# A hybrid decoder layer: four slices of feed-forward operand sums, one PSUM ring order and one set of output rows in other places

## The chip, the cores and the metric

The kernel is one program on one core of one Trainium2 chip. The metric is device time in microseconds (us) of that core, from the start of the program to its end. Lower is better. The kernel before took 2840.08, 2844.31 and 2846.90 us in three runs, with a median of 2844.31 us.

## The reference, cut to what matters

One step of one layer, for 2048 new prompt tokens and 32 sample tokens (8 sequences of 4). The model width is 1024, in fp32 throughout.

```python
def _layer(x, pos, ck, cv, s0, w_in, lb, hg_norm_w, sinks, w_up_a, w_up_b, w_o, n1, n2, w_ff1, w_ff2):
    h = _rmsnorm(x, n1)
    z = h @ w_in
    hq, hf, hi, hg, sq, sk, sv, ga, gb = jnp.split(z, ...)
    f = lb + (1.0 - lb) * jax.nn.sigmoid(hf)
    o_hg, s_new = _hgrn_recurrence(heads(hq), heads(jnp.log(f)), heads(1.0 - f), heads(hi), s0, 64)
    o_hg = _rmsnorm(o_hg, hg_norm_w)
    y_a = (o_hg * jax.nn.silu(hg)) @ w_up_a
    q, k, v = _rotary(sq, pos), _rotary(sk, pos), sv
    o_b, nk, nv = _swa_prompt(q, k, v, sinks)      # or _swa_sample with the cached keys ck and values cv
    y_b = o_b @ w_up_b
    m = jax.nn.sigmoid(ga) * y_a + jax.nn.sigmoid(gb) * y_b
    x = x + m @ w_o
    h2 = _rmsnorm(x, n2)
    x = x + jnp.square(jax.nn.relu(h2 @ w_ff1)) @ w_ff2
    return x, nk, nv, s_new
# y = _rmsnorm(x, normf_w) of both token groups; also returned: the new key and value windows and states
```

`hq`, `hf`, `hi` and `hg` have 512 columns each (4 heads of 128), `sq` 512 (8 heads of 64), `sk` and `sv` 128 each, `ga` and `gb` 1024 each; `w_ff1` is 1024 x 4096 and `w_ff2` 4096 x 1024. Attention goes over a window of 128 positions, with a sink in the softmax.

## The kernel before, in words

**Numbers.** Every fp32 product is made of three fp32r products: each operand is split into a high part (a copy on ScalarE, ACT; L257 in `split_out`, L151 in `split_in`) and a low part (a subtraction on VectorE, DVE; L258 and L152), and TensorE (PE) adds high x high, high x low and low x high in PSUM.

**Blocks and pairs.** The prompt is worked off in 4 blocks of 512 tokens; block 3 also carries the 32 sample tokens (T = 544). Blocks 0 and 1 are the first pair (`sb` = 0, half width `Ths` 512), blocks 2 and 3 the second (`sb` = 1, half width 528). The tokens lie along the free axis, the model's 1024 rows in 8 groups of 128 (`k` or `j`).

**A block.** Blocks 0 and 1 project their columns of `w_in` one after the other (`hi`, `hq`, `sq`, `skv`, and so on); the weight comes in units of two groups of 128 rows (`gemm_NK`: one unit is loaded, split and multiplied, then a hook is called). Block 2 first does `skv` and `sq` for its own tokens, whose result goes over the tiles `stg` to a DRAM buffer `zqk`, and then the **z stage**: all other projections but `hi` for blocks 2 and 3 together, by Strassen's method with seven products (below). After that blocks 2 and 3 load their part of `z` back, and do only `hi` (and block 3 its `sq` and `skv`) by themselves. Then come the window attention, interleaved by hand with the levels of the HGRN2 recurrence (`T_` rotates and transposes a tile, `S_` makes its scores, `P_` turns the probabilities, `V_` multiplies the values; `fill` issues so many matmuls of the recurrence between them), the gate loops (one over `j` for `gb` and `y_b`, "b" below, and one for `ga` and `y_a`, "a"), and `wo`, the product with `w_o`, with a list `todo` of small jobs that are called between its matmuls. In block 2, `wo`'s list holds `reload` and `recast`, which bring block 3's input back and split it. The last pieces of a block, its second norm (`n2.stat`: transposes and row sums of the squares; `n2.spread`: the factor put back on all partitions; `h2_out`: the scaled rows stored), are put into the list `late` and called by hooks (`late_at`) inside the next block's first products.

**The sample tokens** in block 3 are attended to inside its `hi`: `smp_scores`, `smp_turn` and `smp_values` hang on the hooks of units 0, 1 and 2. Their cached keys are loaded into the tile `kc` (L966), behind sixteen small stores of the new sample keys and values (L964).

**Strassen stages.** `strassen_T` runs the z stage and each pair's FF1. A `Wpair` loads a pair of weight columns (`early` the first two operands B11 and B21, `rest` the others) and splits them (`done`). A `Unit` multiplies: `a` does `fB` (into the ring `mm` or `tp`) and `fC` (into `hg`), `b` and `c` the other five, with `fD` in `sw`. The first six units run their `a` ahead of everything else. FF2 goes through seven `steps`; in each, the partial results of four groups of output rows go into PSUM banks that the table `rings` names, and `evac` (L1591) adds them to `y`.

**FF operand sums.** FF1 of the first pair needs S1 to S4, sums of the four quarters of the normed rows. For group `k`, a **slice** is: four loads of 128x512 (`ff_rows`, L583, on SP's queue) into three tiles of the tag `t4`, four sums on DVE (L602 to L608 in `ff_sums`) and four stores (L610, issued from GpSimd, POOL). Four slices make the whole. Before, slices 0 and 1 hang on the hooks of block 2's `hi` (`fr_hook`), slices 2 and 3 on those of block 3's `sq` and `skv` (`sq_fr`).

**What is shared.** PSUM has four rings of two banks, `mm`, `tp`, `hg` and `sw`. Weights go through twelve tiles of tag `w`, three for a unit (raw, high, low). The tag `t4` has three tiles, used by the slices and by the sample's `kc`, `kcT`, `vc` and `pc`. SP's queue issues the weight loads (L138), the slices' loads, `kc` and the small stores; POOL's queue issues the slices' stores and POOL also does the rotary products and the adds of the gates (L1305); ACT's queue issues the stores of `zqk` and of the z stage.

**What sets the order.** The program text is traced in order, and a list scheduler then orders the instructions of each engine by its own estimates. Two things bind it: in the attention part the order on PE is written out by hand, and `pin` (`keep_in_program_order`) keeps an instruction behind everything that was traced before it on its engine. The loads of the slices (L583) and their sums in blocks 2 and 3 are pinned.

**The end.** The second pair's FF2 ends with two pieces of 264 columns, `f1s[0]` and `f1s[1]` (class `Fin`). Each takes squares (`sq`), a statistic over PE (`stat`), the factor spread back over PE (`spread`), and eight output rows (`out`, L1445), each scaled on DVE and stored.

The functions that the diff touches, as they were:

## Time and profile before

| | before |
|---|---|
| median of three runs | 2844.31 us |
| profiled execution | 2856.07 us |
| its span in the trace | 2854.1 us |
| mean granted TensorE clock | 0.987 |
| TensorE (PE) busy | 2743.9 us, 96% |
| TensorE weight loads (PEld) busy | 2414.4 us, 85% |
| VectorE (DVE) busy | 1788.6 us, 63% |
| ScalarE (ACT) busy | 1110.6 us, 39% |
| GpSimd (POOL) busy | 489.8 us, 17% |
| moved by DMA | 487.60 MB, mean 171 GB/s |
| instructions | 50092 |

All of these but the first row are of one execution, taken by the hardware profiler. PE is TensorE's matrix products, and PEld its weight loads, which lie beside them. A wait of an engine is its idle time in front of an instruction, and the profile puts it down to the work that ended last before the instruction could start: "PE x <- ACT y" says that a matmul into tile x stood until ACT was done with y. SPq is the queue of SP, which issues DMAs. The granted clock is the share of TensorE's full clock that it got in a stretch of time. Where a row begins with two numbers, these are the start in us from the beginning of the span and the time in us of one instruction (or of the whole group, where the row ends in a count); a row of the list of waits ends in the sum of us, the number of waits and the longest.

### The profile page before, as it was taken

How to read it: one execution, taken by the hardware profiler on the slowest of the kernel's cores; microseconds unless marked ns; L12 is line 12 of the kernel's file. 1: busy time of each engine (PE TensorE's matmuls, PEld its weight loads, DVE VectorE, ACT ScalarE, POOL GpSimd, SP SyncE). 2: the span in 40 equal slices, each digit the busy share in tenths (PEclk: the TensorE clock that was granted, in tenths of full speed). 3: DMA queues.
4: the chain of work that ended last, by engine and by line, in shares of the span. 5: the costliest groups of instructions: out<-in, count | busy, mean ns of one | idle time of the engine just before them, and what ended most of it. 6: DMA issues, size and time to landing. Idle time of an engine off the chain costs nothing.

```text
span 2854.1 us, 50092 instructions
## 1 busy us (share of the span) xinstructions
PE 2743.9 (96%) x20053; PEld 2414.4 (85%) x20053; DVE 1788.6 (63%) x2905; ACT 1110.6 (39%) x2070; POOL 489.8 (17%) x782
## 2 busy tenths in 40 slices
PE   8999999999899989989899999999998999999998
PEld 7778877788799967767898888887888999999997
DVE  5675646646764375535667777765567777664556
ACT  4542445323344353324325333434443233343332
...
GB/s 187 76 107 236 206 190 67 105 235 264 231 122 113 158 91 106 211 169 51 87 196 208 161 162 159 228 320 230 195 195 205 157 144 152 146 288 187 188 187 114
DMA packets 344481, 487.60 MB, mean 171 GB/s; under 512 B 23432, under 2 KB 220824, under 8 KB 344248
## 3 DMA queue, kind: packets, MB, share of 16 engines
...
## 4 chain that ended last, share of the span: by engine, by line
PE 76%; DMA 8%; DVE 5%; issue 5%; ACT 3%; POOL 2%; SPq 0%; POOLq 0%; ACTq 0%; DVEq 0%
PE f L1585 6%; PE f L1584 6%; PE f L1586 6%; PE fB_f L264 4%; PE fB_f L266 4%; PE fB_f L265 4%; PE fD_f L264 2%; PE fD_f L266 2%; PE fD_f L265 2%; PE wob L1394 1%; PE wob L1392 1%; PE wob L1393 1%; PE fB_z L264 1%; PE fB_z L266 1%; PE fB_z L265 1%
## 5 line engine op out<-in xcount | busy, mean ns | idle before, releaser
L1584 PE MATMUL f<-f2S,hw2T 128*128 128x264 f32 (+1 forms) x576 | 184.5, 320 | 2.5 <-ACT hw2T L151 2.5
L1586 PE MATMUL f<-f2S,lw2T 128*128 128x264 f32 (+1 forms) x576 | 184.2, 320 | 1.0 <-DVE lw2T L152 1.0
L1585 PE MATMUL f<-f2S,hw2T 128*128 128x264 f32 (+1 forms) x576 | 184.1, 320 | 0.0
L264 PE MATMUL fB_f<-S,w1T_f 128*128 128x264 f32 (+1 forms) x384 | 123.0, 321 | 3.1 <-ACT c_f L327 2.5
L1584 PE MATMUL f<-f2A,h_w2B 128*128 128x264 f32 (+1 forms) x384 | 122.4, 319 | 0.0
L1585 PE MATMUL f<-f2A,h_w2B 128*128 128x264 f32 (+1 forms) x384 | 122.3, 319 | 0.0
L1586 PE MATMUL f<-f2A,l_w2B 128*128 128x264 f32 (+1 forms) x384 | 122.3, 318 | 0.0
L265 PE MATMUL fB_f<-S,w1T_f 128*128 128x264 f32 (+1 forms) x384 | 122.2, 319 | 0.0
L266 PE MATMUL fB_f<-S,w1T_f 128*128 128x264 f32 (+1 forms) x384 | 121.9, 319 | 0.0
L152 DVE TENSOR_TENSOR lw2T<-lw2T,hw2T 128x1024 fp32r<-128x1024 f32 x64 | 78.2, 1224 | 65.9 <-ACT hw2T L151 65.0
L1584 PEld LDWEIGHTS f<-f2S,hw2T 128*128 128x128 f32 x576 | 108.7, 189 | 10.5 <-ACT hw2T L151 3.0
L151 ACT CAST hw2T<-lw2T 128x1024 fp32r<-128x1024 f32 x64 | 67.2, 1051 | 128.8 <-DMA lw2T<-w_T 128.8
L1586 PEld LDWEIGHTS f<-f2S,lw2T 128*128 128x128 f32 x576 | 108.4, 188 | 9.5 <-DVE lw2T L152 1.8
L1585 PEld LDWEIGHTS f<-f2S,hw2T 128*128 128x128 f32 x576 | 108.8, 189 | 7.5
L1394 PE MATMUL wob<-m_b,l_wob 128*128 128x512 f32 (+2 forms) x320 | 112.1, 350 | 2.8 <-DVE l_wob L258 2.8
L1392 PE MATMUL wob<-m_b,h_wob 128*128 128x512 f32 (+2 forms) x320 | 112.1, 350 | 0.0
L1393 PE MATMUL wob<-m_b,h_wob 128*128 128x512 f32 (+2 forms) x320 | 111.8, 349 | 0.0
L152 DVE TENSOR_TENSOR f2S<-f2S 128x1024 fp32r<-128x1024 f32 (+1 forms) x64 | 79.0, 1240 | 43.8 <-ACT f2S L151 43.2
L258 DVE TENSOR_TENSOR w1T_f<-w1r_f,w1T_f 128x512 fp32r<-128x512 f32 x128 | 87.4, 688 | 26.2 <-ACT w1T_f L257 25.9
L257 ACT CAST w1T_f<-w1r_f 128x512 fp32r<-128x512 f32 x128 | 77.1, 619 | 65.2 <-PE fB_f L266 27.9
...
L258 DVE TENSOR_TENSOR l_w2B<-rw2B,h_w2B 128x1024 fp32r<-128x1024 f32 x48 | 58.8, 1224 | 62.6 <-ACT h_w2B L257 52.7
...
## 6 DMA issues: line engine op xcount, KB each, us to landing
...
```

What stands on the lines that cost most here:

```text
L152: pin(nc.vector.tensor_tensor(lo, F(lo), F(hi), ALU.subtract), on)
L257: pin(nc.scalar.copy(dh, src), on)
L258: pin(nc.vector.tensor_tensor(dl, src, F(dh), ALU.subtract), on)
L264: nc.tensor.matmul(ps, wh, ah, start=(first and k == 0), stop=False, skip_group_check=not first)
L265: nc.tensor.matmul(ps, wh, al, start=False, stop=False, skip_group_check=not first)
L266: nc.tensor.matmul(ps, wl, ah, start=False, stop=(last and k == 3), skip_group_check=not first)
L1392: nc.tensor.matmul(p, wh, ah, start=(k == 0), stop=False)
L1393: nc.tensor.matmul(p, wh, al, start=False, stop=False)
L1394: nc.tensor.matmul(p, wl, ah, start=False, stop=(k == KD - 1))
L1584: nc.tensor.matmul(ps, wh, ah, start=first, stop=False, skip_group_check=cont)
L1585: nc.tensor.matmul(ps, wh, al, start=False, stop=False, skip_group_check=cont)
L1586: nc.tensor.matmul(ps, wl, ah, start=False, stop=lastk, skip_group_check=cont)
```

## The change

Eleven things are edited together:

1. Slices 0 and 1 leave the hooks of block 2's `hi`. Their loads and sums are called from its gate loops, by a small table: load 0 after `j` = 0 of loop "b", its sums after `j` = 5, load 1 after `j` = 6, its sums after `j` = 3 of loop "a".
2. Slices 2 and 3 leave block 3's `sq` and `skv`. They go into the list `todo` of block 2's `wo`, between `reload` and `recast`.
3. In block 3's `hi`, `smp_turn` moves from unit 1's hook to unit 2's and `smp_values` from unit 2's to unit 3's.
4. In the attention's order by hand, the two `fill`s around the first `P_` change from 30 and 10 to 24 and 16.
5. In block 2, `sq` comes ahead of `skv`. The store of each `stg` is issued with `skv`'s part, and the hooks of `late` change with the order (`late_at(0, 2)` in `sq`, `late_at(1)` in `skv`; before, `late_at(1)` in `skv` and `late_at(0, 1)` in `sq`).
6. The first pair's FF2 uses for the four groups of its last step the rings mm, mm, hg, hg in place of hg, hg, mm, mm.
7. The last block's `n2` uses the ring `sw` in place of `hg`.
8. At the end, the output rows of the first piece `f1s[0]` leave the list `end0`. They are called behind the second piece's statistic, and are pinned there.
9. Follows from 1 and 2: each slice's loads, sums and stores now run in block 2's gate loops and `wo`.
10. In `strassen_T`, the first pair's `early` splits are pinned (`early(i == 0)`).
11. Follows from all: the order on each engine is planned anew for the new text.

`ff_sums` and `fr_sums` also get an argument for the queue of the stores, whose default is the queue used before; no call sets another.

```diff
--- before.py
+++ after.py
@@ -273,16 +273,16 @@
         def __init__(u, N, n, src, wt):
             u.N, u.n, u.src, u.wt, u.ops = f"{N}_{n}", n, src, wt, {}
 
-        def done(u, name, raw):
+        def done(u, name, raw, on=False):
             v = (u.wt if name in ("T3", "T4") else wtile)(F32R, f"w1{name}_{u.N}").rearrange("p (s k c) -> p s k c", s=2, k=4)
-            split_out(v[:, 0], v[:, 1], raw)
+            split_out(v[:, 0], v[:, 1], raw, on)
             u.ops[name] = v
 
-        def early(u):
+        def early(u, on=False):
             v = wtile(F32, f"w1r0_{u.N}").rearrange("p (s k c) -> p s k c", s=2, k=4)
             for kh in range(2):
                 nc.sync.dma_start(v[:, kh], u.src(u.n, kh)[:, 0:P].rearrange("(k p) c -> p k c", p=P))
-                u.done(f"B{kh + 1}1", v[:, kh])
+                u.done(f"B{kh + 1}1", v[:, kh], on)
 
         def rest(u):
             b = []
@@ -380,7 +380,7 @@
             units[-1].free, units[-1].ring = True, mm_ps
         for i in range(ahead):
             if i % nch == 0:
-                units[i].pair.early()
+                units[i].pair.early(i == 0)
             units[i].a(i < 4)
             early(i, units[i])
         for i, u in enumerate(units):
@@ -582,7 +582,7 @@
         for x, (r0, c0) in zip(r, ((0, 0), (4, 0), (0, Th), (4, Th))):
             pin(nc.sync.dma_start(x, h2d[b][(r0 + k) * P:(r0 + k + 1) * P, c0:c0 + Th]))
 
-    def ff_sums(b, v, r, k, loaded=False):
+    def ff_sums(b, v, r, k, loaded=False, q=nc.gpsimd):
 
 
         Th = Ths[b]
@@ -607,7 +607,7 @@
         pin(tt(a21, a11, a21, ALU.subtract), loaded)
         pin(tt(a12, a12, s2, ALU.subtract), loaded)
         for n, x in (("S2", s2), ("S1", s1), ("S3", a21), ("S4", a12)):
-            nc.gpsimd.dma_start(sd[b][n][k * P:(k + 1) * P, :], x)
+            q.dma_start(sd[b][n][k * P:(k + 1) * P, :], x)
 
     def op_load(b, v, x, r0, c0, now=True):
         out = []
@@ -828,13 +828,13 @@
 
             def st_skv(ps, kind, c, nr):
                 nc.scalar.copy(stage[c][:, 512:768], ps)
+                nc.scalar.dma_start(zqk[sb][c * P:(c + 1) * P, :], stage[c])
 
             def st_sq(ps, kind, c, nr):
                 nc.scalar.activation(qk_out(stage[c][:, 0:512]), qk_in(ps), AF.Copy, scale=HD ** -0.5)
-                nc.scalar.dma_start(zqk[sb][c * P:(c + 1) * P, :], stage[c])
-
+
+            colN512(C_SQ, f"sq{B}", st_sq, late_at(0, 2))
             colN(C_SQ + 512, f"skv{B}", st_skv, late_at(1))
-            colN512(C_SQ, f"sq{B}", st_sq, late_at(0, 1))
             Th = Ths[sb]
             r0, r1 = z_half
             A = {"A11": hT_cur[0], "A12": hT_cur[1], "S1": opT(sb, 2, "zS1"), "S2": opT(sb, 3, "zS2"), "S3": opT(sb, 6, "zS3")}
@@ -902,9 +902,11 @@
             fr.append((k, [x[:, c:c + 512] for x in r for c in (0, 512)]))
             ff_rows(0, fr[-1][1], k)
 
-        def fr_sums():
+        def fr_sums(q=nc.gpsimd):
             k, r = fr.pop()
-            ff_sums(0, None, r, k, True)
+            ff_sums(0, None, r, k, True, q)
+
+        fr_at = {("b", 0): lambda: fr_load(0), ("b", 5): fr_sums, ("b", 6): lambda: fr_load(1), ("a", 3): fr_sums} if zs and not odd else {}
 
         if not zs:
             colN512(C_HI, f"hi{B}", ev_v, *((late_at(0, 2, 3), None) if bi else (first_stat, first_split)))
@@ -912,24 +914,13 @@
                 first = bi == 0 and h < 2
                 colT(C_HQ, h, f"hq{B}{h}", ev_q, sw_ps if first else mm_ps, (lambda: spread(rb0, rs0[:, 0], bt, "first")) if first and h == 0 else None)
         if odd or not zs:
-            sq_late = late_at(0, 2, 3)
-            sq_fr = iter([lambda: fr_load(2), none, none, lambda: [fr_sums(), fr_load(3)], none, none, none, fr_sums, none] if zs else [none] * 9)
-            colN512(C_SQ, f"sq{B}", ev_sq, lambda i, ul: [sq_late(), next(sq_fr)()])
-            colN(C_SQ + 512, f"skv{B}", ev_skv, lambda: next(sq_fr)())
+            colN512(C_SQ, f"sq{B}", ev_sq, late_at(0, 2, 3))
+            colN(C_SQ + 512, f"skv{B}", ev_skv)
         else:
             for c in range(ncb):
                 nc.gpsimd.dma_start(qkv[:, c, :], zqk[sb][c * P:(c + 1) * P, :])
             nc.gpsimd.dma_start(qW, kmaj(zd[sb], 0, HH, z0 + ns, bt))
-            def fr_hook(i, ul):
-                if i == 0:
-                    fr_load(0)
-                elif i == 2:
-                    fr_sums()
-                    fr_load(1)
-                elif i == 3:
-                    fr_sums()
-
-            colN512(C_HI, f"hi{B}", ev_v, fr_hook)
+            colN512(C_HI, f"hi{B}", ev_v)
         ob = op(6, F32R, "ob_" + B)[:, 0:8 * T].rearrange("p (s k t) -> p s k t", s=2, k=4)
 
         def rotary_T(ti, nr, rr, r0, name):
@@ -1037,7 +1028,7 @@
 
         if zs and odd:
             nc.gpsimd.dma_start(qW, kmaj(zd[sb], 0, HH, z0 + ns, bt))
-            smp_at = {0: lambda: [smp_scores(kv) for kv in range(NKV)], 1: lambda: [smp_turn(kv) for kv in range(NKV)], 2: smp_values} if smp else {}
+            smp_at = {0: lambda: [smp_scores(kv) for kv in range(NKV)], 2: lambda: [smp_turn(kv) for kv in range(NKV)], 3: smp_values} if smp else {}
             colN512(C_HI, f"hi{B}", ev_v, lambda i, ul: smp_at[i]() if i in smp_at else None)
 
         kts = {-1: k_last}
@@ -1128,7 +1119,7 @@
                     n -= 1
 
         T_, S_, P_, V_ = swa_turn, swa_scores, swa_probs, swa_values
-        for f, c in ((T_, 0), (fill, 6), (S_, 0), (T_, 1), (fill, 12), (S_, 1), (T_, 2), (fill, 30), (P_, 0), (fill, 10), (V_, 0), (S_, 2), (T_, 3), (fill, 10), (P_, 1),
+        for f, c in ((T_, 0), (fill, 6), (S_, 0), (T_, 1), (fill, 12), (S_, 1), (T_, 2), (fill, 24), (P_, 0), (fill, 16), (V_, 0), (S_, 2), (T_, 3), (fill, 10), (P_, 1),
                      (fill, 10), (V_, 1), (S_, 3), (fill, 10), (P_, 2), (fill, 8), (V_, 2), (fill, 16), (P_, 3), (fill, 8), (V_, 3)):
             f(c * len(segs) if f is fill else c)
         fill(1000)
@@ -1277,6 +1268,8 @@
             if zs and j < 4:
                 nc.vector.tensor_copy(ga[:, 2 * j, 0:1], pb[:, j, 0:1])
                 nc.gpsimd.dma_start(ga[:, 2 * j:2 * j + 2, :], kmaj(zd[sb], HH + KD + 2 * j, 2, z0, T))
+            if ("b", j) in fr_at:
+                fr_at["b", j]()
             if sb == 0 and j % 2 == 1:
                 sum_next()
             elif sb == 0:
@@ -1304,6 +1297,8 @@
             for t0, n, o in gate(C_GA, j, ua, a_acts, lambda j, t0, n: ga[:, j, t0:t0 + n] if zs else t2(f"ta_{B}{j}_{t0}")[:, 0:n], "a"):
                 (nc.vector if j >= KD - 2 else nc.gpsimd).tensor_tensor(o, o, pb[:, j, t0:t0 + n], ALU.add)
                 split_out(mT[j // 4][:, 0, j % 4, t0:t0 + n], mT[j // 4][:, 1, j % 4, t0:t0 + n], o)
+            if ("a", j) in fr_at:
+                fr_at["a", j]()
 
         while side.get(bi):
             side_next(bi)
@@ -1354,7 +1349,8 @@
             def recast(g, k):
                 split_in(hT_next[g][:, 0, k:k + 2], hT_next[g][:, 1, k:k + 2], True)
 
-            todo += [lambda: [reload(0, 0), reload(0, 2)], none, lambda: recast(0, 0), lambda: [recast(0, 2), reload(1, 0)], lambda: reload(1, 2), lambda: recast(1, 0), lambda: recast(1, 2)]
+            todo += [lambda: [fr_load(2), reload(0, 0)], lambda: reload(0, 2), fr_sums, lambda: [fr_load(3), recast(0, 0)],
+                     lambda: [recast(0, 2), reload(1, 0)], lambda: [fr_sums(), reload(1, 2)], lambda: recast(1, 0), lambda: recast(1, 2)]
         else:
             Tn = Ths[sb + 1]
             hT_next = [opT(sb + 1, g, "hT") for g in range(2)]
@@ -1409,7 +1405,7 @@
                 nc.gpsimd.dma_start(h2d[sb][k * P:(k + 1) * P, z0:z0 + T], x1[:, k])
 
         if last_b:
-            n2.ring = hg_ps
+            n2.ring = sw_ps
         late += [n2.stat, n2.spread] + ([] if last_b else [h2_out])
     wk_ctx.close()
     cm_ctx.close()
@@ -1438,11 +1434,11 @@
             f.rb = f.x("rb")
             spread(f.rb, f.rs, f.ln, f.N, f.ring)
 
-        def out(f, *js):
+        def out(f, *js, on=False):
             for j in js:
                 y = f.y(j)
                 o = y if f.o is None else f.o()
-                nc.vector.scalar_tensor_tensor(o, y, nfc[:, j:j + 1], f.rb, ALU.mult, ALU.mult)
+                pin(nc.vector.scalar_tensor_tensor(o, y, nfc[:, j:j + 1], f.rb, ALU.mult, ALU.mult), on)
                 f.q.dma_start(yT[j * P:(j + 1) * P, f.c0:f.c0 + f.ln], o)
 
     f1 = None
@@ -1521,7 +1517,7 @@
         if len(chunks) == 1:
             late_ops = []
             ra, rb = (tp_ps, tp_ps, hg_ps, hg_ps), (mm_ps, mm_ps, sw_ps, sw_ps)
-            rings = (ra, rb, rb, ra, rb, rb, (hg_ps, hg_ps, mm_ps, mm_ps))
+            rings = (ra, rb, rb, ra, rb, rb, (mm_ps, mm_ps, hg_ps, hg_ps))
         else:
             rings = ((tp_ps, hg_ps, mm_ps, sw_ps),) * 6 + ((hg_ps, mm_ps, sw_ps, hg_ps),)
         last = sb == nsb - 1
@@ -1644,7 +1640,7 @@
             avs = [u_load(ao, g) for g in range(KG)]
             todo = [lambda: f0.sq(4), lambda: f0.sq(5), lambda: f0.sq(6), lambda: f0.sq(7), none, none, f0.stat, none, none, none, f0.spread]
             todo += [lambda j=j: f0.out(j) for j in range(KD)] + [lambda j=j: [f.sq(j) for f in f1s] for j in range(4, KD)]
-            end0 = [none, none, none, f1s[0].stat, none, f1s[0].spread, lambda: f1s[0].out(0, 1, 2, 3), lambda: f1s[0].out(4, 5, 6, 7)]
+            end0 = [none, none, none, f1s[0].stat, none, f1s[0].spread]
             for jp in range(2):
                 wts = []
                 for g in range(KG):
@@ -1666,6 +1662,7 @@
             while todo:
                 todo.pop(0)()
             f1s[1].stat()
+            f1s[0].out(*range(KD), on=True)
             f1s[1].spread()
             f1s[1].out(*range(KD))
 
```

## The prediction

> **What bounds the kernel now.** The page comes first: TensorE (PE) is busy for almost the whole span, so what another engine does shows in the time only where PE waits for it.
>
> ```profile
> span 2854.1 us, 50092 instructions
> PE 2743.9 (96%) x20053; PEld 2414.4 (85%) x20053; DVE 1788.6 (63%) x2905; ACT 1110.6 (39%) x2070; POOL 489.8 (17%) x782
> ```
>
> The idle part is 2854.1 - 2743.9 = 110.2 us, and the change removes no arithmetic: it can win back idle time, and time in which PE ran at a lower granted clock behind an idle stretch. So the list of PE's waits is next (what waited, for whom, us in total, times, longest). These are the rows that the edits point at, with one for comparison (`c_f`) from a stage that they leave alone:
>
> ```profile
> PE sp_b2c L1070 <- ACT kt_b2c L953: 9.2, 1, 9.2
> ```
>
> ```profile
> PE kcT L973 <- DMA kc<-cache_swa_k: 8.0, 1, 8.0
> PE fB_f L264 <- ACT c_f L327: 6.0, 3, 3.5
> PE fB_f L264 <- DVE y L1591: 4.6, 1, 4.6
> PE pTs L1019 <- DVE ss L1014: 4.0, 1, 4.0
> ```
>
> ```profile
> PE fB_z L264 <- ACT stg L833: 2.8, 1, 2.8
> PE fC_z L264 <- DVE p_z L342: 2.6, 1, 2.6
> ```
>
> ```profile
> PE n_fb L216 <- DVE p_f L342: 2.1, 1, 2.1
> ```
>
> ```profile
> PE po_b1c L1117 <- DVE sm_b1c L1090: 1.7, 1, 1.7
> ```
>
> The rows of the later fences are from the same list, asked for the z stage, the first FF1's start and block 1 alone.
>
> Third, the table by stage, for the stretch behind the larger of these waits. The column before the last two is the granted clock:
>
> ```profile
> 766.00:784.00 18.00, 13.89 (x111) 13.68 (x112) 8.15 (x16) 7.62 (x16) 3.10 (x5) 1.00 0.79 261
> 1012.00:1018.00 6.00, 5.90 (x45) 5.48 (x46) 2.58 (x5) 2.98 (x8) 0.00 (x0) 0.72 0.15 57
> 1258.00:1263.00 5.00, 5.00 (x20) 3.66 (x21) 1.23 (x1) 2.08 (x3) 0.00 (x0) 0.68 0.48 127
> 1282.00:1290.00 8.00, 7.37 (x22) 5.05 (x23) 1.58 (x3) 1.47 (x4) 0.00 (x0) 0.59 0.00 0
> 1550.00:1557.00 7.00, 6.75 (x25) 5.46 (x26) 5.60 (x10) 3.62 (x5) 3.63 (x2) 0.76 0.47 163
> 2163.00:2169.00 6.00, 5.65 (x26) 5.68 (x27) 4.69 (x8) 4.18 (x9) 0.00 (x0) 0.50 0.47 159
> ```
>
> A wait thus costs more than its length. Length of the stretch times (1 - clock) gives 1.7, 1.6, 3.3, 1.7 and 3.0 us for the last five, and nothing for the first. [...]
>
> **The change part by part**, as gains against the profiled execution.
>
> *1. Two slices of FF sums out of block 2's `hi`.* SP's queue carries the weight loads (L138) and the four loads of a slice (L583), in order. The waits of SP from 960 to 1040, then that of ACT from 1000 to 1012:
>
> ```profile
> SPq L583 <- DMA z<-c_z: 10.9, 1, 10.9
> SPq L583 <- DMA dS<-fr: 8.8, 1, 8.8
> ```
>
> ```profile
> ACT h_hgb L257 <- DMA r_hgb<-w_in: 7.7, 1, 7.7
> ```
>
> The loads hold SP, the weights `r_hgb` start late, ACT stands at their cast, and the copy `kt` that the first scores need is behind that cast. With the slices elsewhere SP reaches the weights earlier. The wait of 9.2 and the clock's 1.7 go: 10.9. I leave 0.5 for ACT's copies between the last `hi` matmul and `kt`: **10.4** (bounds 0 and 10.9).
>
> *2. The other two slices out of block 3's `sq`.* SP waited there for buffers of tag `t4` too (its waits from 1200 to 1260), and `kc` shares that tag and that queue:
>
> ```profile
> SPq L583 <- DMA dS<-fr: 7.6, 1, 7.6
> ```
>
> ```profile
> 1245.35 3.80 SPq L964 DMA_DIRECT2D out_new_k_sample<-kv_new  x8
> 1249.19 2.67 SPq L964 DMA_DIRECT2D out_new_v_sample<-kv_new  x8
> 1253.71 0.42 SPq L966 DMA_DIRECT2D kc<-cache_swa_k  x1
> ```
>
> With the buffers free, `kc` can be loaded before it is wanted: 8.0 + 1.6 = 9.6. If it stays behind the sixteen small stores (3.80 + 2.67 = 6.5 us on SP), it comes forward only as far as they can; I leave half of their time, about 3 us, as the lower bound's wait. The first is likelier, as nothing else holds it: **8.5** (bounds 5 and 9.6).
>
> *3. `smp_turn` and `smp_values` one unit of `hi` later.* A unit is thirty matmuls. In the row from 1282, 22 took 7.37 us at clock 0.59, so thirty at full clock take about 30 x 7.37 x 0.59 / 22 = 5.9 us, an estimate, and more than the wait of 4.0. The wait and the clock's 3.3 go: **7.0** (bounds 0, if the probabilities move along, and 7.3).
>
> *4. Fills 30, 10 to 24, 16.* The sum of fills is the same; `po_b1c` has six more matmuls ahead of it after its transposes. 1.7 is at stake, the smaller waits of the other blocks are not counted: **1.2** (bounds -1.7 and 1.7, the transposes now coming sooner after their softmax).
>
> *5. `sq` ahead of `skv` before the z stage.* The last PSUM reads before the stage are now the shorter ones of `skv` on `mm`, and the four stores of `stg` leave one by one. They matter by this row of ACT (what it waited for in brackets):
>
> ```profile
> 779.74 0.94 ACT L327 COPY p_z<-fB_z 128x264 f32<-128x264 f32 x3 [7.87 <-DMA zqk<-stg]
> ```
>
> At stake is 2.8 + 2.6 = 5.4. Against it, `h2_out` (the last of `late`) moves later, into `skv`, and `zS3` needs its buffer. **3.4** (bounds -3 and 5.4).
>
> *6. The last rings of the first pair's FF2 as (mm, mm, hg, hg).* FF1's first matmul wants an `mm` bank. DVE's waits from 2150 to 2170, and its rows:
>
> ```profile
> DVE w1B_f L258 <- ACT w1B_f L257: 5.3, 2, 3.9
> ```
>
> ```profile
> 2158.39 0.68 DVE L1591 TENSOR_TENSOR y<-f,y 128x512 f32<-128x512 f32 x1
> ...
> 2162.52 0.69 DVE L1591 TENSOR_TENSOR y<-f,y 128x512 f32<-128x512 f32 x1
> ```
>
> The evacuations stand behind splits that waited for their weights. With `mm` first, `fB` can start after the first, at 2159.1, and not after the third, at 2163.2: 4.1 earlier. But `fC` wants `hg`, which is now that third, so `fC` is late next. `fB` is twelve matmuls; from the last row of the table they take about 12 x 5.65 / 26 = 2.6 us at half clock and 1.3 at full. Before, `fC` came 2.6 after 2163.2; now it comes at 2163.2, behind a wait of some 2.8: 2.6 won, and of the clock's 3.0 a third: **3.5** (bounds 0 and 4.6 + 3.0 = 7.6).
>
> *7. The last block's statistic on `sw`.* The wait for `hg` (2.1, clock 1.7) goes; its spread now takes both `sw` banks, for which the sixth unit's `fB` then waits for an ACT copy (0.3 us each in part 5's row) and what ACT has ahead of it; 1.5 as an estimate: **2.3** (bounds 0 and 3.8).
>
> *8. First piece's output rows behind the second piece's statistic.* The chain, a PE row and the last DVE row:
>
> ```profile
> 2838.79 3.32 DVE y L1445 x8
> ...
> 2844.72 0.17 DVE rs_y L218
> ```
>
> ```profile
> 2843.52 0.50 PE L216 MATMUL n_y<-ident,xo 128*88 128x128 f32 x3 [2.23 <-DVE xo L1431]
> ```
>
> ```profile
> 2847.11 3.32 DVE L1445 SCALAR_TENSOR_TENSOR y<-y,cols,xo 128x264 f32<-128x264 f32 x8 [2.22 <-ACT xo L229]
> ```
>
> PE is done at 2843.52 - 2.23 = 2841.29, the evacuation waits for DVE until 2838.79 + 3.32 = 2842.1: 0.5 is won. But then the first piece's 3.3 us of rows start at 2844.9 - 0.5 = 2844.4 and end at 2847.7, and the second's start there and not at 2847.1 - 0.5 = 2846.6. The end moves by 2847.7 - 2847.1: **-0.6** (bounds 0.5, and -3.3 if sixteen stores in a row pile up).
>
> *9. The four slices in their new places.* Each is four loads, four DVE sums and four POOL-issued stores:
>
> ```profile
> 995.58 0.69 DVE L605 TENSOR_TENSOR fr<-fr 128x512 f32<-128x512 f32 x1 [10.37 <-DMA fr<-h2d]
> ```
>
> ```profile
> 996.57 2.47 POOL L610 DMA_DIRECT2D dS<-fr  x4 [3.14 <-DVE fr L605]
> ```
>
> That is 4 x 0.69 = 2.8 us of DVE and 2.5 us of POOL a slice, in block 2's gate loops and `wo`, where PE's list has hardly a wait and four PSUM banks let DVE lag by a few us. On SP the `wo` weights queue behind the pinned loads. DVE's and POOL's work lies beside PE's: **-3.0** for small waits (bounds 0 and -43.6, below).
>
> *10. Pinned first splits.* In front of the first FF1:
>
> ```profile
> 1535.51 0.40 PE L264 MATMUL fB_f<-A,w1B_f 128*128 128x512 f32 x1
> ```
>
> ```profile
> 1537.86 2.36 DVE L152 TENSOR_TENSOR S<-S 128x1024 fp32r<-128x1024 f32 x2 [0.21 <-ACT S L151]
> ```
>
> The pinned split must follow those `S` splits, so the first unit can't start before 1540.2 + 0.7 (a subtraction of 128x512, as L605's) = 1540.9. The other units' splits are free, so PE can take the second unit first: **-1.0** (bounds 0 and -5.4 - 3.0 here).
>
> *11. A new plan.* The order on each engine is planned anew, and waits like the 6.0 of `c_f` depend on it: **-3.0** (bounds +6 and -6).
>
> **The sum.** 10.4 + 8.5 + 7.0 + 1.2 + 3.4 + 3.5 + 2.3 = 36.3; less 0.6 + 3.0 + 1.0 + 3.0 = 7.6: 28.7 us. The profiled execution took 2856.07 us (span 2854.1 and 1.97 around it), 0.41% above the median of 2844.31, so the gain is taken as a share: 2827.4 / 2856.07 = 0.990, and 0.990 x 2844.31 = 2816.
>
> **The rivals.**
>
> *A. POOL is held by the moved sums.* POOL's adds in block 2's gate loop took
>
> ```profile
> 1153.02 1.29 POOL L1305 TENSOR_TENSOR ga_b<-ga_b,pb_b 128x512 f32<-128x512 f32 x1 [2.06 <-DVE ga_b L1267]
> 1156.36 2.20 POOL L1305 TENSOR_TENSOR ga_b<-ga_b,pb_b 128x512 f32<-128x512 f32 x1 [2.05 <-DVE ga_b L1267]
> ```
>
> so some grow by 0.9. A slice there could hold POOL for 2.8 + 2.5 us, and `m` and `wo` with it: 5 us more, 2821. [...] Against: `wo` takes `m` by k, so the late ones are wanted last.
>
> *B. Part of the SP wait moves along.* The second and fourth slice's loads again wait for the stores of the one before (8.8 and 7.6 above), weights behind them are late, and two PE waits of 10.9 come back: 28.7 + 3.0 - 21.8 = 9.9 us, 2834. Against: there `wo`'s weights are loaded ahead.
>
> *C. The waits of parts 1 and 2 stay,* because the weights wait for their own buffers. The change then doesn't do what it says: 28.7 - 18.9 = 9.8 us, 2835. Against: ACT's wait is put down to the load itself.
>
> *D. PE keeps the pinned unit first.* Three stage starts at 8.4 each: 28.7 + 1.0 - 25.2 = 4.5 us, 2840.
>
> *E. Slower: SP blocked by all four slices.* Pinned loads can't be passed over, and if each costs PE 10.9, it is 28.7 + 3.0 - 43.6 = -11.9 us, 2856. It decides from the third slice on (32.7 against 31.7).
>
> **How the numbers follow.** Forecast 0.56; A 0.08, B 0.13, C 0.05, D 0.10, E 0.08. About 0.2% (5.7 us) is what a measurement here tells from no change. A, B, C and the better part of D (0.04) are faster: 0.86. The rest of D is the same: 0.06. E is slower: 0.08. The likeliest case's own range is 2800 (the gains of parts 1 to 7 in full, 46.3, and part 8) to 2826 (the rest of part 11's loss, 3.0, and parts 4 to 7 at 3.4 in place of 10.4). The range goes on to 2836 for B and C; D and E, 0.18, are left out.
>
> **What would show it.** Right: no row above 2 us for `sp_b2c`, `kcT`, `pTs`; `n_fb` gone; `fB_f` after `y` under 1.5 with a new `fC_f` row; clock 1.00 from 1000 to 1290 less the time won; the last DVE rows twice 3.3 us back to back. Wrong: SP waits at L583 in the gate loops with a PE wait on `uab` or `wob`; a wait at a stage's first `fB`; new waits in the second FF1.

## The result, and the profile after

The changed kernel takes 2821.56 us (median of four runs, 2816.53 to 2825.65) against 2842.2 for the kernel before, in runs taken together. The ratio is 0.9924, with a 95% interval of 0.9902 to 0.9946: 0.76% or 21.6 us faster. 2816 was forecast from the older median of 2844.31, a ratio of 0.990. The head of the changed kernel's page:

```profile
span 2821.3 us, 50089 instructions
PE 2736.2 (97%) x20053; PEld 2408.2 (85%) x20053; DVE 1791.2 (63%) x2905; ACT 1109.7 (39%) x2070; POOL 490.8 (17%) x782
```

The idle part fell from 110.2 us to 2821.3 - 2736.2 = 85.1, and PE's busy time by 7.7, at a clock of 0.991 against 0.987. The spans differ by 32.8 us, the medians by 20.6: the traced execution of before lies 14 us above that kernel's median. A second trace of it, told below, has a span of 2844.7, 23.4 above the changed kernel's.

From the list of PE's waits after the change (what waited, for whom, us in total, times, longest; `carry` is the running sum of squares that the statistic `n_fb` turns):

```profile
PE yab L167 <- DVE l_uab L258: 3.8, 1, 3.8
PE wob L1388 <- ACT h_wob L257: 3.4, 2, 1.7
PE n_fb L216 <- DVE carry L245: 2.0, 1, 2.0
PE ps_sqb_-1_11574 L191 <- ACT h_sqb L257: 1.3, 1, 1.3
PE fC_f L264 <- DVE c_f L342: 1.3, 1, 1.3
...
PE kcT L964 <- ACT SV_b L940: 0.3, 1, 0.3
```

`sp_b2c`, `pTs`, `po_b1c`, `fB_z` and `fB_f` behind `y` have no row any more, and `kcT` is at 0.3 in place of 8.0. `yab` waited 0.8 for `l_uab` before, `wob` not for `h_wob` and `sq` not at all; `n_fb` waited 2.1 for `p_f`, and `fC_f` 1.2 for `c_f`. What came instead stands in block 2's gate loops and `wo` and in the head of block 3's `sq`, where the four slices now are. The list of SP's waits there (1040 to 1200 us), and the table by stage (start and end, length, PE, PEld, DVE, ACT and POOL busy, granted clock, DMA share, GB/s):

```profile
SPq L583 <- DMA dS<-fr: 48.8, 4, 22.5
...
SPq L957 <- DMA dS<-fr: 12.8, 1, 12.8
```

```profile
1003.00:1010.00 7.00, 6.85 (x35) 5.36 (x35) 6.96 (x15) 4.05 (x16) 0.00 (x0) 1.00 0.33 97
1128.00:1140.00 12.00, 8.16 (x28) 6.27 (x28) 8.95 (x12) 2.80 (x4) 4.86 (x6) 0.86 0.65 209
1150.00:1160.00 10.00, 8.23 (x28) 6.02 (x27) 4.53 (x4) 3.98 (x5) 2.89 (x3) 0.83 0.24 91
1505.00:1520.00 15.00, 14.42 (x54) 11.50 (x53) 12.39 (x17) 11.68 (x17) 4.77 (x5) 0.77 0.90 300
```

The four waits of L583 are those of the second, third and fourth slice, for the stores of the slice before; the first slice's loads wait at most 1.3 us, for PE. L957 is `kc`, which waits for the last slice's stores and is issued at 1186.04, well before PE wants it at 1238.

The clock behind `sp_b2c` is whole again (1.00). The dips to 0.86 and 0.83 are new; the one to 0.77 stands where the first trace of before had 0.76 over 7 us.

The 3.8 us of `yab` are not SP's: the high part of its weights was cast by 1128.0, and DVE took the low part (L258) only after the four pinned sums of a slice, from ACT's and DVE's timelines:

```profile
1126.95 1.04 ACT L257 CAST h_uab<-r_uab 128x1024 fp32r<-128x1024 f32 x1
...
1129.49 1.76 DVE L607 TENSOR_TENSOR fr<-fr,fr 128x512 f32<-128x512 f32 x1
1131.17 0.68 DVE L608 TENSOR_TENSOR fr<-fr,fr 128x512 f32<-128x512 f32 x1
1131.77 1.21 DVE L258 TENSOR_TENSOR l_uab<-r_uab,h_uab 128x1024 fp32r<-128x1024 f32 x1
```

**The stages, trace by trace.** One pair of traces mixes the edits with the luck of two executions. So each stage was measured in every trace, from the start of the first matmul into one tile to that into another, by the timelines of PE, in us. The column "undone" is the changed kernel with that one part undone (its experiment is told below). Some stages without an edit hardly vary: block 2's `hi` takes 25.7 in all traces, and block 1 from `gb` to `wo` 148.3 to 148.6. (In the second pair's FF1 ten units of 264 columns run their `a` ahead, not six; the 11th `fC_f` is the first of a unit that does not.)

```
stage (from -> to)                      before, two traces   changed   undone
block 1: kT -> gb               part 4      85.1   83.4        80.2     85.0
block 1's wo -> first fC_z      part 5      88.9   88.6        86.7     89.0
                                part 10                                 89.4
first fC_z -> block 2's hi      part 10    206.3  206.0       201.9    205.7
block 2: kT -> sp               part 1      11.0   10.1         1.6      9.8
block 2: sp -> lv               part 4      41.4   41.9        37.9     42.2
                                part 1                                  40.3
block 2's y_b -> 3's rb_fb      part 9     128.3  128.3       144.4    128.3
block 3: kT_smp -> hi           part 2      12.0   11.9         2.8     11.4
block 3: hi -> kT_b3c           part 3      42.5   39.3        34.2     40.4
block 3: kT_b3c -> lv           part 3      46.1   46.0        42.7     45.5
                                part 4                                  44.7
block 3's wo -> rb_fb           part 7      80.4   79.1        82.4     84.5
                                part 10                                 76.5
n_y -> second FF1's 11th fC_f   part 6     149.1  144.6       145.2    145.1
last FF2 matmul's end -> end    part 8      12.8   12.8        13.8     13.2
```

Two stages vary with no part. Block 2's `lv` to `y_b` took 46.0 and 48.1 before, 42.6 in the changed kernel and 41.8 to 48.0 in the others. The first pair's FF2, up to its statistic, took between 274.0 and 281.4. Falls of the clock explain a part of it: in both stages they take nothing in some traces and up to 3.4 us in others (last section).

### The profile page after: what moved, and what is told of

It reads as the page before. It is cut to its first block, busy times and chain, and to the rows that moved or that the text cites. A ratio compares the mean times of both kernels' runs of the same rounds, so it can differ in the third digit from the quotient of the medians.

```text
span 2821.3 us, 50089 instructions
## 1 busy us (share of the span) xinstructions
PE 2736.2 (97%) x20053; PEld 2408.2 (85%) x20053; DVE 1791.2 (63%) x2905; ACT 1109.7 (39%) x2070; POOL 490.8 (17%) x782
## 4 chain that ended last, share of the span: by engine, by line
PE 80%; DMA 5%; issue 5%; DVE 5%; ACT 3%; POOL 2%; SPq 0%; DVEq 0%; POOLq 0%; ACTq 0%
PE f L1581 6%; PE f L1580 6%; PE f L1582 6%; PE fB_f L264 4%; PE fB_f L266 4%; PE fB_f L265 3%; PE fD_f L264 2%; PE fD_f L266 2%; PE fD_f L265 2%; PE ps_hfb L684 2%; PE wob L1390 2%; PE wob L1388 2%; PE wob L1389 2%; PE fB_z L264 1%; PE fB_z L266 1%
## 5 line engine op out<-in xcount | busy, mean ns | idle before, releaser
L1580 PEld LDWEIGHTS f<-f2S,hw2T 128*128 128x128 f32 x576 | 108.7, 189 | 11.1 <-ACT hw2T L151 3.5
L1582 PEld LDWEIGHTS f<-f2S,lw2T 128*128 128x128 f32 x576 | 108.4, 188 | 10.6 <-DVE lw2T L152 2.9
L258 DVE TENSOR_TENSOR w1T_f<-w1r_f,w1T_f 128x512 fp32r<-128x512 f32 x128 | 87.3, 688 | 26.0 <-ACT w1T_f L257 25.7
L1507 POOL DMA_DIRECT2D u_S<-s_f x144 | 77.7, 541 | 110.5 <-DVE s_f L1502 93.1
```

The costliest lines, as they stand in the source:

```text
L258: pin(nc.vector.tensor_tensor(dl, src, F(dh), ALU.subtract), on)
L1507: nc.gpsimd.dma_start(us[o][u.n // 4][u.n % 4 * P:(u.n % 4 + 1) * P, u.t0:u.t0 + u.ln], y_)
L1580: nc.tensor.matmul(ps, wh, ah, start=first, stop=False, skip_group_check=cont)
L1582: nc.tensor.matmul(ps, wl, ah, start=False, stop=lastk, skip_group_check=cont)
```

## The experiments

**A second trace of the kernel before.** No edit.

> The kernel before, unchanged, for a second trace: its first profiled execution took 2856.07 us, where its runs took 2840 to 2847. Theory: the waits that the change aims at are the program's own, so kt of sp_b2c (9.2 us), kc (8.0), ss of pTs (4.0) and y of the second FF1 (4.6) come back within 1 us, and the 9 to 16 us between the executions lie in the granted clock (0.987 there) and small waits. Rival: one of them is that execution's own, and is below half here; then the comparison of the two traces credits the change with what it did not do.

Its profiled execution took 2846.64 us. `kt` came back at 8.4, `kc` at 7.4 and `ss` at 3.3, and `fB_z` and `y` as follows:

```profile
PE fB_z L264 <- ACT stg L833: 2.3, 1, 2.3
PE fB_f L264 <- DVE y L1591: 2.1, 1, 2.1
```

So the large ones are the program's own. The rival holds for two small terms: the wait on `y` is below half of the 4.6 that part 6 was costed with, and `fC_z` behind `p_z` (2.6) is down to 0.2.

**The slices put back.**

```diff
-            colN512(C_HI, f"hi{B}", ev_v)
...
+            colN512(C_HI, f"hi{B}", ev_v, fr_hook)
...
-            if ("b", j) in fr_at:
-                fr_at["b", j]()
...
```

> The changed kernel with the four slices put back to block 2's hi and block 3's sq (parts 1, 2 and 9 undone). Theory (the two traces, read by stage): parts 1 and 2 won 12.4 + 9.2 = 21.6 us and part 9 cost 16.1, so the slices are worth 5.5 net: about 2827 us, with waits of about 9 for sp_b2c and 8 for kcT again and no wait above 1 on yab, wob or sqb. Rival 1 (the forecast's price of 3.0 for part 9): the slices are worth 15.9, about 2838. Rival 2 (the new waits on yab, wob and sqb come from the new plan and not from the slices): they stay, and the time is about 2843.

2828.19 us, ratio 0.9944 (0.9924 to 0.9963). `sp_b2c` waits 8.2 and `kcT` 7.2 again; no wait above 0.8 is left on `yab`, and the stretch of part 9 is back at 128.3. So the slices are worth some 0.20% of 2842.2, 5.7 us, as the theory has it; the two intervals together leave some 8 us to either side, here and in the comparisons below, so the sizes rest on the stages. Parts 1 and 2 by stage: 9.8 - 1.6 + 40.3 - 37.9 = 10.6, and 11.36 - 2.82 = 8.5. Part 9: 144.4 - 128.3 = 16.1 lost; in the other kernels with the slices in these places the stretch takes 141.1 to 143.3, so 13 to 16. Of the 16.1, 67.6 - 63.1 = 4.5 lie in the gate loops, where `yab` waits for DVE, and 11.6 in `wo` and `sq`.

**The slices alone,** in the kernel before.

```diff
-            colN512(C_HI, f"hi{B}", ev_v, fr_hook)
+            colN512(C_HI, f"hi{B}", ev_v)
...
+            if ("b", j) in fr_at:
+                fr_at["b", j]()
...
```

> The kernel before with parts 1, 2 and 9 alone. Theory (stage by stage reading): 12.4 + 9.2 won, 16.1 lost: 5.5 us faster, about 2837 against 2842. Rival 1 (forecast): 15.9 faster, about 2826. Rival 2 (the slices win nothing here, since the waits of sp_b2c and kcT are not theirs): within 2 us of before or slower.

2840.85 us, ratio 0.9986 (0.9972 to 0.9999), some 4 us faster. The forecast's 15.9 is excluded. The time alone doesn't exclude rival 2, the stages do: part 9's takes 141.4, `kT` to `sp` 1.6 and `kT_smp` to `hi` 2.8.

**The slices without the wait for buffers.**

```diff
-        a11, a12, a21, a22, s1, s2 = r
+        a11, a12, a21, a22 = r[:4]
+        s1, s2 = (a22, a11) if loaded else r[4:]
...
+                    fr0.append(op(0, F32, "frs"))
...
+        fr_at = {("b", 0): lambda: fr_load(0), ("b", 2): fr_sums, ("b", 3): lambda: [fr_load(1, 0), fr_load(2, 1)], ("b", 6): fr_sums, ("a", 0): fr_sums, ("a", 1): lambda: fr_load(3), ("a", 4): fr_sums} if zs and not odd else {}
```

> The changed kernel, with the slices' loads freed from waiting for the stores of the slice before: the sums are taken in place (four regions of 512 a slice in place of six), slices 1 and 2 go into slot 0, free in block 2's gate loops, slices 0 and 3 into two tiles of t4, and all four are done in the gate loops. Theory (the loads block SP's queue, and the weights behind them are late): the waits of SP at L583 go, and with them those of yab, wob and sqb; 10 to 16 us faster than the changed kernel: 2806 to 2812. Rival 1 (DVE's four pinned sums, 2.8 us a slice, are what holds l_uab and the x_b rows): the waits on l_uab and wob stay, 2818 to 2824. Rival 2: the queue blocks until slot 0 is free, and the time is above 2824.

2817.74 us, ratio 0.9904 (0.9883 to 0.9924): a step, but less than expected, and the time alone lies at rival 1's edge. The stages separate them: from `wo` to block 3's `rb_fb` it is 65.7, as before the change (65.2) and not 76.8 as in the changed kernel, but the gate loops grew from the changed kernel's 67.6 to 73.4. One load still waits on SP, with the weights of `yab` behind it:

```profile
SPq L583 <- DMA dS<-fr: 33.9, 1, 33.9
```

```profile
PE yab L165 <- ACT h_uab L257: 4.9, 2, 3.1
```

**The last slice's loads later.** The last slice comes in `wo`'s list, the third slice's sums after `j` = 1.

```diff
-        fr_at = {("b", 0): lambda: fr_load(0), ("b", 2): fr_sums, ("b", 3): lambda: [fr_load(1, 0), fr_load(2, 1)], ("b", 6): fr_sums, ("a", 0): fr_sums, ("a", 1): lambda: fr_load(3), ("a", 4): fr_sums} if zs and not odd else {}
+        fr_at = {("b", 0): lambda: fr_load(0), ("b", 2): fr_sums, ("b", 3): lambda: [fr_load(1, 0), fr_load(2, 1)], ("b", 6): fr_sums, ("a", 1): fr_sums} if zs and not odd else {}
...
-            todo += [lambda: [reload(0, 0), reload(0, 2)], none, lambda: recast(0, 0), lambda: [recast(0, 2), reload(1, 0)], lambda: reload(1, 2), lambda: recast(1, 0), lambda: recast(1, 2)]
+            todo += [lambda: [fr_load(3), reload(0, 0), reload(0, 2)], none, lambda: recast(0, 0), lambda: [recast(0, 2), fr_sums(), reload(1, 0)], lambda: reload(1, 2), lambda: recast(1, 0), lambda: recast(1, 2)]
```

> As the kernel with the slices in slot 0, but the last slice's loads come at the start of wo's list, ahead of the reload, and its sums with recast(0, 2); the third slice's sums come after j = 1 of loop a. In that kernel the last slice's loads still stood 33.9 us on SP for the first slice's stores, with the weights of yab behind them (waits on h_uab 4.9, l_uab 1.8). Theory (the wait for buffers on SP's queue is the cost): the loads now come to SP after those stores, no wait of SP at L583 above 10 and none of PE on yab above 1, and the time is 5 to 9 us under that kernel's 2818: 2809 to 2813. Rival (DVE's and POOL's work in the gate loops is the cost, whatever SP does): waits on l_uab, m and wob stay, 2816 to 2820.

2813.15 us, ratio 0.9885 (0.9867 to 0.9903). SP's wait at the loads for stores is down to 0.4, and the part's stretch is 137.4. `yab`, against the theory, waits 5.3 for `l_uab`. The timeline of ACT, DVE and POOL shows that the rival has its share:

```profile
1122.01 1.05 ACT L257 CAST h_uab<-r_uab 128x1024 fp32r<-128x1024 f32 x1
...
1127.06 0.68 DVE L609 TENSOR_TENSOR frs<-frs 128x512 f32<-128x512 f32 x1
1127.66 2.28 DVE L258 TENSOR_TENSOR l_uab<-r_uab,h_uab 128x1024 fp32r<-128x1024 f32 x1
...
1135.28 1.22 DVE L258 TENSOR_TENSOR l_uab<-r_uab,h_uab 128x1024 fp32r<-128x1024 f32 x1
...
1127.40 1.47 POOL L1306 TENSOR_TENSOR ga_b<-ga_b,pb_b 128x512 f32<-128x512 f32 x1
```

The high part is there at 1123.1, but DVE takes the low part only at 1127.66, behind the pinned sums, and then needs 2.28 us where the same form takes 1.22 at 1135.28. POOL's add ends at 1128.87, so waiting for it would make 1.21 + 1.22 = 2.43, and half speed beside it 1.22 + 1.21 / 2 = 1.8. The row is 0.15 us under the first and 0.5 over the second. Two rows of other traces are alike: in the changed kernel a subtraction of this form takes 1.99 at 1153.74, where POOL's add to `carry` ends 0.90 later, and in the first trace of before POOL's add takes 2.20 at 1156.36, where such a subtraction on DVE ends 1.06 later, and 1.29 at 1153.02, with no work of DVE beside it. The one that starts second takes 1.06, 0.77 and 0.91 us longer in these three rows, of the 1.21, 0.90 and 1.06 that the two lie side by side.

**The parts that win.** As the last kernel; the third slice's sums come behind the last split of `yab`'s weights, the reload into slot 0 comes one call later, and the first splits are pinned in the z stage alone (why is told with the free splits, below).

```diff
-        fr_at = {("b", 0): lambda: fr_load(0), ("b", 2): fr_sums, ("b", 3): lambda: [fr_load(1, 0), fr_load(2, 1)], ("b", 6): fr_sums, ("a", 1): fr_sums} if zs and not odd else {}
+        fr_at = {("b", 0): lambda: fr_load(0), ("b", 2): fr_sums, ("b", 3): lambda: [fr_load(1, 0), fr_load(2, 1)], ("b", 6): fr_sums, ("a", 4): fr_sums} if zs and not odd else {}
...
-                units[i].pair.early(i == 0)
+                units[i].pair.early(i == 0 and N[0] == "z")
...
-            todo += [lambda: [fr_load(3), reload(0, 0), reload(0, 2)], none, lambda: recast(0, 0), lambda: [recast(0, 2), fr_sums(), reload(1, 0)], lambda: reload(1, 2), lambda: recast(1, 0), lambda: recast(1, 2)]
+            todo += [lambda: fr_load(3), lambda: [reload(0, 0), reload(0, 2)], lambda: recast(0, 0), lambda: [recast(0, 2), fr_sums(), reload(1, 0)], lambda: reload(1, 2), lambda: recast(1, 0), lambda: recast(1, 2)]
```

> The kernel whose last slice loads late, with two more edits: the third slice's sums come after j = 4 of loop a (behind the last split of yab's weights on DVE, where the pinned sums stood ahead of l_uab: 5.3 of PE's wait), the reload into slot 0 comes one call later, and the first splits are pinned in the z stage alone (free, they won 5.8 us at the first FF1's start and lost about 6 from block 1's end to the z stage's). Theory: no wait above 1 on yab, 4 won there, 4 to 6 at the first FF1: 2802 to 2806 against 2813. Rival 1 (the pin's loss at the first FF1 is the wait on carry, which stays): 2807 to 2810. Rival 2 (slot 0 comes free too late for the reload, and the weights of wo are late): 2813 or more.

2809.61 us, ratio 0.9878 (0.9857 to 0.9899); the time is rival 1's, the mechanism rival 2's. `yab` waits 0.9, from `y_b` to `wo` takes 63.6 (63.1 before the change), and the first FF1 starts as expected (76.5). But `wo` has grown to 54.3. SP stands at the reload into slot 0, which comes free later, and ACT waits for `wo`'s weights behind it (SP from 1060 to 1200, ACT from 1130 to 1190):

```profile
SPq L1355 <- DMA dS<-frs: 20.2, 1, 20.2
```

```profile
ACT h_wob L257 <- DMA r_wob<-w_o: 16.5, 2, 9.2
```

**The reload later.**

```diff
-            todo += [lambda: fr_load(3), lambda: [reload(0, 0), reload(0, 2)], lambda: recast(0, 0), lambda: [recast(0, 2), fr_sums(), reload(1, 0)], lambda: reload(1, 2), lambda: recast(1, 0), lambda: recast(1, 2)]
+            todo += [lambda: fr_load(3), none, lambda: [reload(0, 0), reload(0, 2)], lambda: [fr_sums(), recast(0, 0)], lambda: [recast(0, 2), reload(1, 0)], lambda: reload(1, 2), lambda: recast(1, 0), lambda: recast(1, 2)]
```

> As the kernel of the parts that win, but the reload into slot 0 comes one call later in wo's list, and the last slice's sums one call earlier. In that kernel SP stood 20.2 us at the reload for the third slice's stores, ACT waited 16.5 for r_wob behind it, and the stretch from wo's first matmul to block 3's sq took 54.3 us against 45.3 before the change; the stretch from ybb to wob was already down from 67.6 to 63.6 (63.1 before). Theory (what is behind the pinned, waiting DMA on SP's queue is the cost): the wait at the reload falls under 12, the stretch takes 45 to 48, and the time is 6 to 8 us less: ratio 0.985 to 0.9855, about 2801 to 2803. Rival (the sums and casts on DVE are the cost in wo): the stretch stays above 51, ratio 0.987 to 0.988.

2807.94 us, ratio 0.9853 (0.9835 to 0.9871), 42 us under the kernel before. The ratio is the expected one, 7 us better than the last kernel's, but that is within the two intervals, and the medians differ by 1.7 us only. The stage decides. The same two rows:

```profile
SPq L1355 <- DMA dS<-frs: 7.0, 1, 7.0
```

```profile
ACT h_wob L257 <- DMA r_wob<-w_o: 4.9, 3, 3.1
```

`wo` takes 46.7, the whole stretch of part 9 63.3 + 46.7 + 20.0 = 130.0, against 137.8 in the last kernel. The same four slices, with as many sums and stores, cost 1.7 us here and 16.1 in the changed kernel. What cost was the place: what stands behind a pinned instruction that waits, on SP above all, and on DVE. No run frees the loads from their pin, so whether that alone would do as well stays open.

**The sample's turn early again.**

```diff
-            smp_at = {0: lambda: [smp_scores(kv) for kv in range(NKV)], 2: lambda: [smp_turn(kv) for kv in range(NKV)], 3: smp_values} if smp else {}
+            smp_at = {0: lambda: [smp_scores(kv) for kv in range(NKV)], 1: lambda: [smp_turn(kv) for kv in range(NKV)], 2: smp_values} if smp else {}
```

> The changed kernel with part 3 undone (smp_turn on unit 1's hook, smp_values on unit 2's). Theory (by stage, the two traces show 8.4 us won between the end of skv and block 3's rotation): 8 slower than the changed kernel, about 2830, with pTs waiting some 4 for ss and the clock near 0.6 behind it. Rival 1 (the wait was there since kcT stood 8 us, and without that the softmax is done in time): no wait on pTs, 2821 to 2823. Rival 2 (the forecast's 7.0): 2828.6; the two sizes can't be told apart by the time alone, but by the stretch.

2827.7 us, ratio 0.9939 (0.9921 to 0.9957). By the time alone the part is worth some 4 us, within the intervals; by stage 6.2, and up to 2.8 in the next, of which 1.7 is a fall of the clock that other kernels have there too. The waits are back, so rival 1 is out, and so is the clock behind them:

```profile
PE pTs L1010 <- DVE mxs L996: 2.3, 1, 2.3
PE pTs L1010 <- DVE ss L1005: 1.1, 1, 1.1
```

```profile
1262.00:1270.00 8.00, 6.57 (x19) 4.13 (x20) 2.44 (x8) 3.35 (x9) 0.00 (x0) 0.57 0.15 46
```

**`skv` first.**

```diff
-            colN512(C_SQ, f"sq{B}", st_sq, late_at(0, 2))
...
             colN(C_SQ + 512, f"skv{B}", st_skv, late_at(1))
+            colN512(C_SQ, f"sq{B}", st_sq, late_at(0, 1))
...
```

> The changed kernel with part 5 undone (skv ahead of sq, the stores in sq). Theory (by stage 6.6 won from block 1's end to block 2's hi, of which 5.1 by the start of fD): 5 to 7 slower, about 2827, and the rows of fB_z behind stg (2.3 to 2.8) and of fC_z behind p_z (2.6) come back. Rival 1 (the forecast's 3.4): 2825. Rival 2 (the row of fC_z isn't in the second trace of the kernel before, so only 2.3 is the order's): 2823 to 2824.

2828.09 us, ratio 0.9936 (0.992 to 0.9952). The time fits the theory too (3.4 us by ratio), but the stage is 2.3 longer, `fB_z` waits 1.7 for `stg`, and the row of `fC_z` behind `p_z` is at 0.2: rival 2. The rest of what the first two traces showed around the z stage isn't part 5's.

**The first splits free.**

```diff
-                units[i].pair.early(i == 0)
+                units[i].pair.early()
...
```

> The changed kernel with part 10 undone (no pinned first splits). In the changed kernel PE stood 2.0 and 0.6 at the first FF1's start and had a clock of 0.77 over 15 us, and that start was 2.2 us worse than before. Theory (the pin keeps the first unit late): the start is 2 to 4 better, fB_f begins ahead of n_fb without a wait, 2818 to 2820; the z stage and the second FF1 start as in the changed kernel. Rival 1 (the wait belongs to the statistic, which waits for carry, whatever the splits do): within 1 us of the changed kernel. Rival 2 (the pin serves the second FF1, and without it the wait after y comes back): 2 to 4 slower.

2826.05 us, ratio 0.9932 (0.9915 to 0.9949). Neither theory nor rivals have the whole: at the first FF1 the pin costs 82.4 - 76.5 = 5.9 us (no wait there now; other kernels with the pin and `sw` take 80.2 to 80.9 there, which makes it 4), and around the z stage, which was expected to stay, it wins 2.7 + 3.8 = 6.5. Ahead of that stage PE waits 2.7 where the changed kernel has 1.4, and ACT shows for what:

```profile
PE ps_skvb L176 <- ACT stg L830: 2.7, 1, 2.7
```

```profile
754.04 0.62 ACT L257 CAST w1B_z<-w1r_z 128x512 fp32r<-128x512 f32 x1 [4.49 <-DMA w1r_z<-w_in]
...
757.07 0.36 ACT L830 COPY stg<-ps_skvb 128x256 f32<-128x256 f32 x1
```

Free, the casts of the z stage's first weights are planned ahead of `skv`'s copies; the weights aren't there yet, and the copies, for whose bank PE waits, stand behind the cast. Pinned, the casts come behind the third copy. Inside the stage PE waits 1.6, 0.5 and 0.4 for evacuations that it doesn't wait for in the changed kernel; that is 2.5 of the 3.8, and the rest stays open.

**The three rings and rows back.** Parts 6, 7 and 8 undone, which lie in different stages.

```diff
-            rings = (ra, rb, rb, ra, rb, rb, (mm_ps, mm_ps, hg_ps, hg_ps))
+            rings = (ra, rb, rb, ra, rb, rb, (hg_ps, hg_ps, mm_ps, mm_ps))
...
-            n2.ring = sw_ps
+            n2.ring = hg_ps
...
```

> The changed kernel with parts 6, 7 and 8 undone (hg first in FF2's last step of the first pair, the last block's statistic on hg, the first piece's rows ahead of the second's statistic). The three lie in different stretches and are read there. Theory from the two traces: at the second FF1's start fB waits 2 to 5 for y again, some 6 lost of which 2 come back by the fourth fC; at the first FF1 nothing changes, as the statistic waits for carry on either ring; the end, from the last matmul of FF2, is 12.8 as before and not 13.8. In all 3 slower, about 2825. Rival 1 (the forecast's 3.5 + 2.3 - 0.6 = 5.2): 2827. Rival 2 (the FF1 is bound by its own waits, fC and fD take what fB wins): 2821 to 2822.

2821.67 us, ratio 0.9916 (0.99 to 0.9931), not slower than the changed kernel: rival 2. At the second FF1 the wait on `y` is back with 1.4 only, and the stage to the eleventh unit's `fC` takes 145.1 against 145.2: the first `fC` comes 1.6 later without part 6, the seventh 0.4. At the first FF1 part 7 is worth 84.5 - 82.4 = 2.1 (4 against the other kernels' 80.2 to 80.9), and the end is 0.6 shorter without part 8.

**The fills back.**

```diff
-        for f, c in ((T_, 0), (fill, 6), (S_, 0), (T_, 1), (fill, 12), (S_, 1), (T_, 2), (fill, 24), (P_, 0), (fill, 16), (V_, 0), (S_, 2), (T_, 3), (fill, 10), (P_, 1),
+        for f, c in ((T_, 0), (fill, 6), (S_, 0), (T_, 1), (fill, 12), (S_, 1), (T_, 2), (fill, 30), (P_, 0), (fill, 10), (V_, 0), (S_, 2), (T_, 3), (fill, 10), (P_, 1),
```

> The changed kernel with part 4 undone (fills 30 and 10). Theory from the two traces: 4.9 us were won in block 1 between the first pT and gbb, and 3.4 in block 3 between the first pT and the lv rows; so 6 to 8 slower, 2828 to 2830, with po_b1c waiting 1.7 for sm and ps_hfb of block 3 2.9 for ACT again. Rival 1 (the forecast's 1.2, the rest being the run's own): 2822 to 2823. Rival 2 (the new plan alone shortened those stretches): within 1 us.

2833.37 us, ratio 0.9961 (0.9945 to 0.9977): 0.37% of 2842.2, or 10.5 us, slower, more than theory and rivals. By stage it is 85.0 - 80.2 = 4.8 in block 1, 42.2 - 37.9 = 4.3 in block 2 and 44.7 - 42.7 = 2.0 in block 3. Two blocks have the same wait, and each has a clock behind it (from 470 and from 1018):

```profile
PE po_b1c L1108 <- DVE sm_b1c L1081: 2.2, 1, 2.2
PE po_b2c L1108 <- DVE sm_b2c L1081: 2.0, 1, 2.0
```

```profile
470.00:476.00 6.00, 6.00 (x43) 2.97 (x40) 3.56 (x7) 1.64 (x5) 0.29 (x1) 0.74 0.01 3
1018.00:1024.00 6.00, 5.86 (x34) 2.36 (x36) 3.16 (x5) 1.33 (x3) 0.29 (x1) 0.72 0.00 0
```

2.2 + 6 x 0.26 = 3.8, and 2.0 + 6 x 0.28 = 3.7: that is most of each block's loss. The fall of the clock doesn't always come: in the kernel with the slices alone, which has the old fills, blocks 1 and 2 have no fall in these stages and take 83.4 and 41.1, each 3.2 over the changed kernel. So the part is worth 3.2 + 3.2 + 2.0 = 8.4 without a fall, and 11.1 in this trace.

## Why the prediction was right, and where its terms were not

The time lies inside the range, 5.6 us above the forecast. That the sum is this close is luck in part: two errors of 10 and 13 us nearly cancel. In us, gain positive, the forecast against the traced execution of before, the measured by stage with the changed kernel's own trace:

```
part                            forecast   measured
1  slices 0, 1 out of hi          10.4       10.6
2  slices 2, 3 out of sq           8.5        8.5
3  sample's turn later             7.0        6.2 (to 9.0)
4  fills 24, 16                    1.2       11.1 (8.4 without falls of the clock)
5  sq ahead of skv                 3.4        2.3 (with part 10 alone)
6  FF2's last rings                3.5        0
7  statistic on sw                 2.3        2.1
8  rows behind the statistic      -0.6       -0.6 to -1.0
9  slices in their new places     -3.0      -16.1
10 pinned splits                  -1.0       -2.1 (3.8 won, 5.9 lost)
11 new plan                       -3.0        0 (no stage shows it)
sum                               28.7       21.8
```

The sum of the stages, with 0.8 for part 8, is 10.6 + 8.5 + 6.2 + 11.1 + 2.3 + 2.1 - 0.8 - 16.1 - 2.1 = 21.8, and the ratio gives 21.6. So close an agreement is chance, as the parts don't simply add. In block 2 parts 1 and 4 make 10.6 + 4.3 = 14.9 one at a time, while the stretch from `kT` to `lv` got 12.5 to 13.0 shorter than in the two traces of before. The stretch ahead of the z stage gets 2.3 or 2.7 longer when part 5 or part 10 is undone, and got 1.9 to 2.2 shorter with both; the table counts it once, under part 5.

*Right.* Parts 1 and 2: the chain from SP's queue over the late weights and ACT's cast to `kt` was read step by step, and the clock behind the wait was counted. It held to 0.2 us. Parts 3, 7 and 8 held in size. Two signs of being right did not come: the clock from 1000 to 1290 is not whole, and `n_fb` is not gone; it waits 2.0 for `carry`, with the pinned splits alone, as there is no such wait where they are free. The rows of both pieces are one group of DVE now:

```profile
2810.30 6.54 DVE L1441 SCALAR_TENSOR_TENSOR y<-y,cols,xo 128x264 f32<-128x264 f32 x16
```

*Part 9 failed,* and it is the largest error: 16.1 in place of 3.0. The step was "DVE's and POOL's work lies beside PE's". In the gate loops it didn't: DVE's pinned sums held the low part of `yab`'s weights, 3.8 us of PE's wait and a fall of the clock, 4.5 in all. And the larger cost, 11.6 in `wo` and `sq`, is mostly SP's queue. Rival B had its mechanism, that the loads wait for the stores of the slice before, and set it at 0.13, "there `wo`'s weights are loaded ahead". Only two of the eight loads of those weights were (at 1112.9 and 1116.4, PE's first product in `wo` at 1139.3): a pinned load goes into SP's order where it was called, and SP comes there well before PE does. B counted the second and the fourth slice, and E all four; three waited, 48.8 us together. The signs stand in the prediction's last list under "wrong".

*Part 4 failed the other way.* The 1.2 counts block 1's wait alone. The order by hand is run by every block, and undoing it costs something in three. In the rows of before, block 2's wait was 1.2 and 1.6 us, in front of it the 9.2 for `kt`; with the slices gone from `hi` and the old fills (the slices alone) it is 1.9 + 0.6 = 2.5. So a part of this gain is there only together with part 1. The clock behind block 1's wait was 1.00 in both traces of before, so no row called for it; the falls in the trace with the old fills are its own.

*Part 6* took a wait of 4.6 that the second trace has at 2.1, and by the eleventh unit of FF1 nothing of it is left: that stage is as long with the one order as with the other. The bound of 0 was the answer. *Part 10:* rival D's mechanism came at one of three stage starts (5.9; D had 8.4 for each). That a pin also keeps a cast without data from standing ahead of copies that PE needs was not thought of. *Part 5* had 2.6 in its stake that was one execution's own.
